# A two-layer trunk in split fp32: the order of parts, sums and products changed in four places

## The chip, the core and the metric

The kernel runs on one core of one Trainium2 chip. The metric is the device time of one execution in microseconds (us). The kernel before takes 1653.25 us, the median of three runs (1652.49 to 1653.59). The profiler records one execution by engine: PE (matrix products), ACT (activations and copies), DVE (elementwise work), POOL (here it only issues DMAs that add into memory) and SP (which issues plain loads and stores).

## The reference

The input x has 512 tokens of 1024 numbers, in fp32. Two layers follow one another:

```python
# layer i, mixer i mod 2
x += 1/2 * ffn_a(rms_norm(x)); x += mixer(rms_norm(x)); x += 1/2 * ffn_b(rms_norm(x))
# ffn: (silu(x @ Wg) * (x @ Wu)) @ W_out, inner width 2816
# mixer 0: recurrent: (gelu(y) * rg_lru(conv4(r))) @ w_out, with y, r = split(x @ w_in)
# mixer 1: spatial gating: (u * (w_s @ rms_norm(v) + b_s)) @ w_out, with u, v = split(gelu(x @ w_in))
# at the end: rms_norm(x)
```

Four feed-forward blocks and two mixers make up nearly all of the work. All of their weight products are 512 tokens by 1024 or by 2816.

## The kernel before

**Split numbers.** A product in fp32 is made of three products in fp32r, a format of fewer bits. Each operand is cut into a high part (`hi` for activations, `whi` for weights) and a low part (`lo`, `wlo`): ACT writes the high part as a copy, and DVE subtracts it from the original to get the low part. Lines 362, 363 and 364 issue the three matmuls of one 128x128 block of activations and 512 columns of weights.

**Seven products for eight.** `seven` (L334) multiplies blocks of 2 by 2 by the method of seven products, P1, P2, P5, P6, P3, P7 and Q4. Each needs one left operand out of A11, A12, S1, S2, S4, S3 and A22 (the S are sums of blocks) and one right operand, a weight block or a sum of blocks. Products add up in PSUM banks named A, B, C and Q: P1, then P6 and P7, use A; P2 uses B; P5 and P3 use C; Q4 uses Q in the output products. Each bank pair is emptied by ACT or DVE before the next product that starts in it anew. Every product is done in cuts, two or so halves of the inner dimension; product and cut together are a "sub", written P6_0 and P6_1 below.

**Weights.** A weight block is loaded by SP into a `raw` tile (`Raw.fetch`, one of 8 buffers). Sums of blocks are made in two ways. POOL can issue an accumulating DMA that adds a second block from memory onto the raw tile (`Raw.add`, L136). This is done either as `plus`, two subs after the load, from the list `pending`, or as `then`, right behind the tile's split, when the tile is used again for the next sum. Or DVE adds another raw tile onto it (`Sub.add`, `tile`), one instruction of 128x1024. A POOL DMA waits in POOL's queue until the tile is there and its last reader is done, and POOL issues strictly in order.

**Order.** The loop at the end of the kernel goes through the subs. For each it runs pending accumulations, hooks set for that sub ("pre", "mid", "rest"), the splits of weights up to three subs ahead, new loads, the matmuls, and the "end" and "late" hooks. Engine queues follow this program order; an instruction that waits holds up all behind it on its engine.

**Left operands.** `left_blocks` (L627) sets the steps of a group: the transposes `e` of a quarter (PE, L264) a number of subs later (`lag`), the evacuation of PSUM into an SBUF tile `a` and its split; then the sums S2, S4, S3 on DVE. `Group.direct` (L285) makes high and low parts straight from PSUM, half by half: hi, lo, hi, lo.

**Opening.** The kernel begins with a pair of 128-wide column blocks done plainly (`pair_plain`), while x is squared and summed for the first norm; `rt`, the norm's scale, is made by ACT and DVE. Then follows the first chunk (`chunk`, sub 8 on), whose B banks come from the two auxiliary banks, which the transposes share. Its c1 (P1 + P2) is added by DVE from bank B, which frees the auxiliary banks.

**Output products.** `out_blocks` (L559) does an output product with the residual addition. Its `parts` hooks make hi and lo of S4 and the like a number of subs ahead of their product (`lead`, 2 as a rule). In the recurrent mixer the order is P1, P5, P2 for either cut, P6, P3 for either cut, then P7 and Q4 for both. `FinalNorm` (L792) gives the order of the very last output product and joins the final norm to it; P3's two cuts are joined there.

Of the kernel before, what the change touches and what calls it, by code (L numbers as in the profile page):

```python
# [13 lines left out]
P = 128  # L14
# [38 lines left out]
def trunk(ctx: ExitStack, tc: tile.TileContext, a: dict, out: bass.AP):  # L53
# [57 lines left out]
    class Raw:  # L111
# [1 line left out]

        halves = False

        def __init__(self, src, shape, plus=None):
            self.src, self.shape, self.plus, self.uses, self.done = src, shape, plus, 0, 0

        def turn(self):
            self.uses += 1  # L120
# [2 lines left out]
        def load(self):  # L123
            _, k, c = self.shape
            t = rawp.tile([P, 1024], F32, tag="raw", name=nm("raw"))
            self.v = t[:, : k * c].rearrange("p (k c) -> p k c", k=k)
            live.add(self)
            self.fetch()
            if self.plus is not None:
                pending.append((now[0] + 2, self))  # L130

        def fetch(self):
            nc.sync.dma_start(out=self.v, in_=self.src)
# [68 lines left out]

    raws = []

    def raw_of(src, shape, plus=None):
        raws.append(Raw(src, shape, plus))
        return raws[-1]

    subs = []
# [35 lines left out]
    class Group:  # L245
# [39 lines left out]
        def direct(self, name, ps, gains):  # L285

            hi, lo = self.hl[name] = slot(F32R, "hi")[:, : self.n * H], slot(F32R, "lo")[:, : self.n * H]
            for q, g in enumerate(gains):
                c = slice(q * H, (q + 1) * H)
                act(hi[:, c], ps[:, c], AF.Copy, scale=g)  # L290
                stt(lo[:, c], ps[:, c], g, f32(hi[:, c]), ALU.mult, ALU.subtract)

        def stage(self, n, name, src, gains=None, parts=True, where=None, direct=0):
# [40 lines left out]
    def seven(block, cuts, left, w, posts, order=None, own=False, apart=False, joined=None, spare=bank):  # L334

        bk, raw, held = {}, {}, []
        banks = dict(BANK, Q4=("Q", True)) if apart else BANK

        def mm_of(prod, ci):
            name, fresh = banks[prod]
            pairs = cuts[ci]

            def mm(sub):
                if fresh and ci == 0:
                    for s in range(2):  # L350
                        bk[name, s] = (spare if name == "B" else bank)(name)[:, :w]
                if prod == joined and ci == 0:
                    held.extend((sub, q, i) for q, i in enumerate(pairs))
                    return
                for s in range(2):
                    ps = bk[name, s]
                    k = {} if fresh else dict(skip_group_check=True)
                    for sb, q, i in (held if prod == joined else []) + [(sub, q, i) for q, i in enumerate(pairs)]:
                        zh, zl = left(prod, i, s)
                        wh, wl = sb.hi[:, q, :], sb.lo[:, q, :]  # L360
                        end = i == cuts[-1][-1]
                        nc.tensor.matmul(ps, zh, wh, start=fresh and i == 0, stop=False, **k)  # L362
                        nc.tensor.matmul(ps, zl, wh, start=False, stop=False, **k)  # L363
                        nc.tensor.matmul(ps, zh, wl, start=False, stop=end, **k)  # L364
                    if ci == len(cuts) - 1 and prod in posts:
                        posts[prod](s, ps)
            return mm

        order = order or [(p, ci) for p in ORDER for ci in range(len(cuts))]

        def far(ci):
            return own and order.index(("P6", ci)) - order.index(("P5", ci)) >= 4

        for prod, ci in order:
            def new(k, n, plus=None):
                b = lambda k, n: block(k, n, cuts[ci])
                return raw_of(b(k, n), [P, len(cuts[ci]), w], plus and b(*plus))

            tile = then = tile_then = None
            if prod == "P1":  # L380
                r = raw[11, ci] = new(0, 0)
            elif prod == "P2":
                r = new(1, 0)
            elif prod == "P5":
                if own:
                    raw[11, ci] = new(0, 0, (0, 1))
                    if far(ci):
                        then = block(1, 1, cuts[ci])
                else:
                    tile = raw[12, ci] = new(0, 1)  # L390
                    tile_then = block(1, 1, cuts[ci])
                r = raw[11, ci]
            elif prod == "P6" and far(ci):
                r, then = raw[11, ci], block(1, 0, cuts[ci])
            elif prod == "P6":
                r, tile, then = raw[11, ci], new(1, 1), block(1, 0, cuts[ci])
                raw[22, ci] = tile
            elif prod == "P3":
                r = new(1, 1) if far(ci) else raw[22, ci]
            elif prod == "P7":  # L400
                r = new(0, 1, (1, 1)) if own else raw[12, ci]
            else:
                r = raw[11, ci]
            subs.append(Sub(r, mm_of(prod, ci), None, tile, then, tile_then))
        return order

# [149 lines left out]
                hook(n + 4, "pre", lambda: self.take(1))  # L556


    def out_blocks(w, k0, groups, scale, norm=None, order=None, own=False):  # L559

        n = [g for g in groups]
        cuts, bases, i, r = [], {}, 0, k0
# [57 lines left out]
        for i, (prod, ci) in enumerate(order):  # L620
            if prod in ("P3", "P6", "P7", "Q4"):
                lead = 6 if ends and prod == "P3" else 4 if isinstance(norm, TileNorm) and prod in ("P7", "Q4") else 3 if 1 in n else 2
                hook(at0 + i - lead, "mid", lambda ci=ci, name=LEFT[prod]: gs[ci].parts(name))
        return gs

# [27 lines left out]
        return left_of(lambda: S.z)  # L653


    def chunk(w_in, f0, nt, group, spare=bank):

        w = nt * P
        c1, c2, c3, c5, ht = {}, {}, {}, {}, {}

        def rt(t):
            return S.rt[:, t : t + 1]

        def new(d, s, name):
            d[s] = slot(name=name)[:, :w]
            return d[s]

        def p1(s, ps):
            act(new(c1, s, "c1"), ps, AF.Copy)

        def p2(s, ps):
            tt(c1[s], c1[s], ps, ALU.add)
            hook(now[0] + 1, "mid", lambda: act(c1[s], c1[s], AF.Silu, scale=rt(s)))

        def p5(s, ps):
            act(new(c5, s, "c5"), ps, AF.Copy)

        def p6(s, ps):
            act(new(c2, s, "c2"), ps, AF.Copy)

        def p3(s, ps):
            tt(c2[s], ps, c2[s], ALU.subtract)
            stt(c2[s], c2[s], rt(s), c1[s], ALU.mult, ALU.mult)
            ht[s] = c2[s]
            if s == 1:
                left_blocks(group, ht, 0)

        def p7(s, ps):
            act(new(c3, s, "c3"), ps, AF.Copy)
            hook(now[0] + 1, "mid", lambda: tt(c5[s], c5[s], c3[s], ALU.subtract))  # L690

        def q4(s, ps):
            s4 = slot(name="s4")[:, :w]
            act(s4, ps, AF.Silu, scale=rt(2 + s))
            stt(c5[s], c5[s], rt(2 + s), s4, ALU.mult, ALU.mult)
            ht[2 + s] = c5[s]
            if s == 1:
                left_blocks(group, ht, 1)

        seven(in_block(w_in, lambda n: n * DFF + f0 * P, w), [[0, 1], [2, 3]], x_left(), w,  # L700
              dict(P1=p1, P2=p2, P5=p5, P6=p6, P3=p3, P7=p7, Q4=q4), spare=spare)

    def pair_plain(w_in, f0, group, first=False):

# [31 lines left out]
        def post(half):  # L736
            for s in range(2):
                ps, t = st[half, s], 2 * half + s
                if t not in ht:
                    silu(half, s)  # L740
                o = slot(name="h")[:, :w]
                stt(o, ps[:, w:], S.rt[:, t : t + 1], ht[t], ALU.mult, ALU.mult)
                ht[t] = o
            left_blocks(group, ht, half, 4 if first else 2)

        at0 = len(subs)
        for i, (half, left) in enumerate(((0, "A12"), (0, "A11"), (1, "A22"), (1, "A21"))):
# [27 lines left out]
    def ffn(w_in, w_out, norm):  # L775
        f0 = 0
        for i, sizes in enumerate(FF_PARTS):
            groups, p0 = [], f0
            for n in sizes:
# [3 lines left out]
                    f0 += 2  # L783
                else:
                    groups.append(Group(n // 2))
                    chunk(w_in, f0, n, groups[-1], aux if len(subs) == 8 else bank)
                    f0 += n
            gs = out_blocks(w_out, p0, [g.n for g in groups], 0.5, norm if i == len(FF_PARTS) - 1 else None, own=True)
            gs.update(enumerate(groups))
# [2 lines left out]
    class FinalNorm:  # L792

        ORDER = [(p, ci) for p in ("P1", "P2", "P5", "P6", "P7", "Q4", "P3") for ci in range(2)]

        def __init__(self):
            self.gain, self.q, self.m, self.s = {}, {}, {}, {}
# [95 lines left out]
    def recurrent(w_in, w_out, norm):  # L895
# [132 lines left out]
        for i, at in enumerate(((11, 12, 15), (13, 14, 16))):  # L1028
            for fn, n in zip((groups[i].s2, groups[i].s4, groups[i].s3), at):
                hook(y0 + n, "pre", fn)  # L1030

        def y_post(c, ps):
            ym[c] = ps
# [31 lines left out]
        order = [(p, ci) for ci in range(2) for p in ("P1", "P5", "P2")]  # L1065
        order += [(p, ci) for ci in range(2) for p in ("P6", "P3")]
        order += [(p, ci) for p in ("P7", "Q4") for ci in range(2)]
        gs = out_blocks(w_out, 0, [2, 2], 1.0, norm, order, own=True)
        gs.update(enumerate(groups))


# [358 lines left out]
                         (4, "rest", lambda: (value(0, "A21"), value(1, "A21")))):  # L1430
        hook(n, phase, fn)
    squares(4, "rest", "A11")
    squares(4, "rest", "A12")
    squares(5, "rest", "A22")
    squares(5, "rest", "A21")
    rstd(6, (0, "rest"), (0, "rest"), (1, "pre"))
    first.rest(1, None)
    hook(20, "end", vec_rest_t)
# [50 lines left out]
```

## Time and profile before

| | us |
|---|---|
| median of three runs | 1653.25 |
| profiled execution | 1653.5 |
| its span | 1651.7 |
| PE busy | 1621.3 (98%) |
| DVE busy | 1361.2 (82%) |
| ACT busy | 1033.6 (63%) |
| POOL busy | 214.1 (13%) |

The span runs from the first to the last instruction that the profiler records; the rest of the execution's time lies around it. Busy shares are means over the whole span. A wait's row gives an engine's total idle time ahead of a kind of instruction, how many times, and the longest. A row of the timeline gives start, duration, engine, source line, operation, and what it writes and reads; in square brackets stand the idle time just before it and what ended it. Matmul durations overlap: the step from start to start is the time that one takes.

HBM moves 165 GB/s on average, and the clock of PE was 0.995 of its full rate.

### The profile page before, as it was taken

What the parts mean: (1) busy time and instruction counts of PE and PEld (TensorE: products, weight loads), DVE (VectorE), ACT (ScalarE), POOL (GpSimd) and SP (SyncE); (2) the same over time, 40 slices, a digit from 0 to 9 for tenths busy, and PEclk for the clock granted to TensorE, in tenths of its full rate; (3) what the DMA queues carried; (4) which work ended last, traced back from release to release, by engine and by line L of the source; (5) the groups of instructions that cost most, each with busy time, mean ns of one, the idle gap of its engine ahead of it and who ended that gap; (6) DMA issues with size and microseconds to landing.
All of it is one profiled execution on the core that took longest, in us unless ns stands there. A gap on an engine that the chain in (4) does not pass through costs nothing.

```text
span 1651.7 us, 20816 instructions
## 1 busy us (share of the span) xinstructions
PE 1621.3 (98%) x7475; PEld 1334.7 (81%) x7475; DVE 1361.2 (82%) x1821; ACT 1033.6 (63%) x1501; POOL 214.1 (13%) x194
## 2 busy tenths in 40 slices
PE   9899999999999999999999999999999999999997
PEld 7688888888878888888888888888788888888885
DVE  6898897887798797877987978778866888879777
ACT  6656556667867556556775565566774865665655
POOL 1111111200010111111101111112101011121110
PEclk9999999999999999999999999999999999999999
DMA  5667966853373876876838768769864557686683
GB/s 211 148 167 177 217 156 165 210 146 102 90 179 92 183 184 174 207 169 161 203 86 191 170 171 208 175 163 217 193 165 104 152 119 187 166 207 168 157 205 79
DMA packets 161560, 273.54 MB, mean 166 GB/s; under 512 B 11328, under 2 KB 37552, under 8 KB 161456
## 3 DMA queue, kind: packets, MB, share of 16 engines
q1 hardware_dynamic: 113856, 182.74, 35.8%
q0 software_dynamic: 45808, 87.63, 31.7%
q10 hardware_dynamic: 1792, 1.84, 0.4%
q8 instruction: 59, 0.97, 0.2%
q14 instruction: 45, 0.37, 0.1%
HBM read 270.07 MB, written 2.10 MB: 165 GB/s over the span
## 4 chain that ended last, share of the span: by engine, by line
PE 87%; DVE 6%; ACT 4%; issue 1%; DMA 1%; SPq 0%; ACTq 0%; DVEq 0%
PE A L362 13%; PE A L363 13%; PE A L364 13%; PE C L363 7%; PE C L364 7%; PE C L362 7%; PE p L727 4%; PE e L264 3%; PE B L362 3%; PE B L364 3%; PE B L363 3%; DVE wlo L87 2%; PE Q L364 1%; PE Q L362 1%; PE Q L363 1%
## 5 line engine op out<-in xcount | busy, mean ns | idle before, releaser
L96 ACT ACTIVATE whi<-raw 128x1024 fp32r<-128x1024 f32 (+1 forms) x530 | 547.0, 1033 | 416.4 <-PE A L363 114.5
L87 DVE TENSOR_TENSOR wlo<-raw,whi 128x1024 fp32r<-128x1024 f32 (+1 forms) x531 | 631.1, 1191 | 207.1 <-ACT whi L96 205.7
L362 PE MATMUL A<-whi,hi 128*128 128x512 f32 x984 | 392.1, 398 | 4.4 <-DVE x L93 4.4
L364 PE MATMUL A<-wlo,hi 128*128 128x512 f32 x984 | 384.9, 391 | 0.0
L363 PE MATMUL A<-whi,lo 128*128 128x512 f32 x984 | 384.5, 391 | 0.2 <-DVE lo L87 0.2
L362 PEld LDWEIGHTS A<-whi,hi 128*128 128x128 f32 x984 | 185.2, 188 | 41.3 <-issue 4.8
L362 PE MATMUL C<-whi,hi 128*128 128x512 f32 x544 | 213.8, 393 | 4.4 <-ACT hi L96 4.4
L364 PEld LDWEIGHTS A<-wlo,hi 128*128 128x128 f32 x984 | 185.1, 188 | 40.3
L363 PEld LDWEIGHTS A<-whi,lo 128*128 128x128 f32 x984 | 185.5, 189 | 37.8 <-DVE lo L87 1.2
L363 PE MATMUL C<-whi,lo 128*128 128x512 f32 x544 | 214.0, 393 | 1.8 <-DVE lo L87 1.5
L364 PE MATMUL C<-wlo,hi 128*128 128x512 f32 x544 | 213.2, 392 | 1.2 <-DVE wlo L87 1.2
L136 POOL DMA_DIRECT2D raw<-in_ffn_w_in_dram x80 | 96.4, 1205 | 750.4 <-DVE raw L87 558.6
L136 POOL DMA_DIRECT2D raw<-in_ffn_w_out_dram x72 | 83.0, 1156 | 390.3 <-DVE wlo L87 155.0
L87 DVE TENSOR_TENSOR raw<-raw,raw 128x1024 f32<-128x1024 f32 (+1 forms) x107 | 128.2, 1199 | 0.5
L87 DVE TENSOR_TENSOR lo<-a,hi 128x512 fp32r<-128x512 f32 (+1 forms) x188 | 122.6, 659 | 3.7 <-ACT hi L96 3.1
L362 PEld LDWEIGHTS C<-whi,hi 128*128 128x128 f32 x544 | 103.0, 189 | 26.9 <-ACT hi L96 5.5
L363 PEld LDWEIGHTS C<-whi,lo 128*128 128x128 f32 x544 | 102.9, 189 | 26.3 <-DVE lo L87 5.1
L364 PEld LDWEIGHTS C<-wlo,hi 128*128 128x128 f32 x544 | 102.9, 189 | 23.0 <-DVE wlo L87 1.7
L96 ACT ACTIVATE hi<-a 128x512 fp32r<-128x512 f32 (+1 forms) x188 | 112.5, 600 | 13.0 <-DVE a L87 10.8
L96 ACT ACTIVATE c<-A 128x512 f32<-128x512 f32 x126 | 74.1, 594 | 57.0 <-PE A L364 56.4
L362 PE MATMUL B<-whi,hi 128*128 128x512 f32 x272 | 109.0, 401 | 0.0
L364 PE MATMUL B<-wlo,hi 128*128 128x512 f32 x272 | 106.5, 391 | 0.6 <-DVE wlo L87 0.6
(170 smaller groups left out, 2202.9 us busy)
## 6 DMA issues: line engine op xcount, KB each, us to landing
raw<-in_ffn_w_in_dram SPq DMA_DIRECT2D x160, 512.0 KB, 4.5
raw<-in_ffn_w_out_dram SPq DMA_DIRECT2D x100, 512.0 KB, 5.4
raw<-in_ffn_w_in_dram POOLq DMA_DIRECT2D x80, 512.0 KB, 7.5
raw<-in_ffn_w_out_dram POOLq DMA_DIRECT2D x60, 512.0 KB, 7.7
raw<-in_sg_w_in_dram SPq DMA_DIRECT2D x18, 512.0 KB, 5.1
raw<-in_rec_w_in_dram SPq DMA_DIRECT2D x16, 512.0 KB, 3.9
raw<-in_ffn_w_in_dram SPq DMA_DIRECT2D x30, 256.0 KB, 4.0
raw<-in_ffn_w_out_dram SPq DMA_DIRECT2D x20, 256.0 KB, 4.8
```

Of the source, the lines that this page charges most:

```text
L87: nc.vector.tensor_tensor(out=o, in0=x, in1=y, op=op)
L96: nc.scalar.activation(out=o, in_=x, func=f, **k)
L136: nc.gpsimd.dma_start(out=self.v, in_=src, accum_op=ALU.add)
L264: nc.tensor.transpose(ps[:, o : o + P], src(q, s), ident)
L362: nc.tensor.matmul(ps, zh, wh, start=fresh and i == 0, stop=False, **k)
L363: nc.tensor.matmul(ps, zl, wh, start=False, stop=False, **k)
L364: nc.tensor.matmul(ps, zh, wl, start=False, stop=end, **k)
L727: nc.tensor.matmul(bank_of(half, s), z, (sub.lo if m == 2 else sub.hi)[:, q, :], start=left[2] == "2" and (h, q, m) == (0, 0, 0), stop=lef ...
```

## The change

The program does the same arithmetic, apart from the order of some sums of weight blocks. Six edits:

1. `Group.direct` writes both high halves first, then both low halves.
2. The last output product of the kernel goes P1, P2, P6, P5, P7, Q4, P3 in place of P1, P2, P5, P6, P7, Q4, P3. Its sums of weights are built to suit: P6 takes a fresh block (0,0) and adds a tile that holds (0,1) + (1,1); P5 goes on with P1's tile plus (0,1); Q4 goes on with P6's; P7 is the tile; P3 loads (1,1) anew. The number of loads and of DVE additions there is the same.
3. In the first chunk, P5 and P7 get tiles of their own: (0,0) and (0,1) are loaded again, and POOL accumulates (0,1) and (1,1) onto them. Two loads and two accumulating DMAs are added, two DVE additions of 128x1024 go.
4. The squares of x in the opening move: A12 from step 4 to 5, A22 and A21 from step 5 to 6.
5. The transposes of the first pair's group come one sub later (`lag` 5 for 4).
6. In the recurrent and part of the spatial output product, P7's accumulation is queued six (or five) subs after its load rather than two, the pending list is kept sorted, and in the recurrent one hi and lo for P3_0 are made a sub earlier (`soon`).

```diff
@@ class Raw
-        def __init__(self, src, shape, plus=None):
+        def __init__(self, src, shape, plus=None, wait=2):
...
             if self.plus is not None:
-                pending.append((now[0] + 2, self))
+                pending.append((now[0] + self.wait, self))
+                pending.sort(key=lambda p: p[0])
@@ Group.direct
-            for q, g in enumerate(gains):
-                c = slice(q * H, (q + 1) * H)
+            cs = [(slice(q * H, (q + 1) * H), g) for q, g in enumerate(gains)]
+            for c, g in cs:
                 act(hi[:, c], ps[:, c], AF.Copy, scale=g)
+            for c, g in cs:
                 stt(lo[:, c], ps[:, c], g, f32(hi[:, c]), ALU.mult, ALU.subtract)
@@ seven
+        def again(ci):
+            return own and order.index(("P5", ci)) - order.index(("P1", ci)) >= 6
...
             if prod == "P1":
                 r = raw[11, ci] = new(0, 0)
+                if again(ci):
+                    then = block(0, 1, cuts[ci])
...
             elif prod == "P5":
-                if own:
+                if again(ci):
+                    pass
+                elif own:
                     raw[11, ci] = new(0, 0, (0, 1))
...
+            elif prod == "P6" and joined:
+                r, tile, then = new(0, 0), new(0, 1, (1, 1)), block(1, 0, cuts[ci])
+                raw[6, ci], raw[12, ci] = r, tile
...
             elif prod == "P3":
-                r = new(1, 1) if far(ci) else raw[22, ci]
+                r = new(1, 1) if far(ci) or joined else raw[22, ci]
             elif prod == "P7":
-                r = new(0, 1, (1, 1)) if own else raw[12, ci]
+                r = raw[12, ci] if joined or not own else new(0, 1, (1, 1), 6 - ci if far(ci) else 2)
             else:
-                r = raw[11, ci]
+                r = raw[6 if joined else 11, ci]
@@ out_blocks
+                lead = soon.get((prod, ci), lead)
@@ chunk
-              dict(P1=p1, P2=p2, P5=p5, P6=p6, P3=p3, P7=p7, Q4=q4), spare=spare)
+              dict(P1=p1, P2=p2, P5=p5, P6=p6, P3=p3, P7=p7, Q4=q4), own=first, spare=aux if first else bank)
@@ pair_plain
-            left_blocks(group, ht, half, 4 if first else 2)
+            left_blocks(group, ht, half, 5 if first else 2)
@@ FinalNorm
-        ORDER = [(p, ci) for p in ("P1", "P2", "P5", "P6", "P7", "Q4", "P3") for ci in range(2)]
+        ORDER = [(p, ci) for p in ("P1", "P2", "P6", "P5", "P7", "Q4", "P3") for ci in range(2)]
@@ recurrent
+        soon = {("P3", 0): 3}
...
-        gs = out_blocks(w_out, 0, [2, 2], 1.0, norm, order, own=True)
+        gs = out_blocks(w_out, 0, [2, 2], 1.0, norm, order, own=True, soon=soon)
@@ opening
     squares(4, "rest", "A11")
-    squares(4, "rest", "A12")
-    squares(5, "rest", "A22")
-    squares(5, "rest", "A21")
+    squares(5, "rest", "A12")
+    squares(6, "rest", "A22")
+    squares(6, "rest", "A21")
```

More of the change, by code (lines that the diff above doesn't have):

```diff
@@ L114, in trunk @@
         halves = False
-        def __init__(self, src, shape, plus=None):
-            self.src, self.shape, self.plus, self.uses, self.done = src, shape, plus, 0, 0
+        def __init__(self, src, shape, plus=None, wait=2):
+            self.src, self.shape, self.plus, self.wait, self.uses, self.done = src, shape, plus, wait, 0, 0
         def turn(self):
@@ L203, in trunk, with raw_of @@
     raws = []
-    def raw_of(src, shape, plus=None):
-        raws.append(Raw(src, shape, plus))
+    def raw_of(src, shape, *plus):
+        raws.append(Raw(src, shape, *plus))
         return raws[-1]
@@ L372, in far, with new @@
             return own and order.index(("P6", ci)) - order.index(("P5", ci)) >= 4
+        def again(ci):
+            return own and order.index(("P5", ci)) - order.index(("P1", ci)) >= 6
         for prod, ci in order:
-            def new(k, n, plus=None):
+            def new(k, n, plus=None, wait=2):
                 b = lambda k, n: block(k, n, cuts[ci])
-                return raw_of(b(k, n), [P, len(cuts[ci]), w], plus and b(*plus))
+                return raw_of(b(k, n), [P, len(cuts[ci]), w], plus and b(*plus), wait)
             tile = then = tile_then = None
@@ L556, in quarter, with out_blocks @@
                 hook(n + 4, "pre", lambda: self.take(1))
-    def out_blocks(w, k0, groups, scale, norm=None, order=None, own=False):
+    def out_blocks(w, k0, groups, scale, norm=None, order=None, own=False, soon={}):
         n = [g for g in groups]
@@ L653, in x_left, with chunk @@
         return left_of(lambda: S.z)
-    def chunk(w_in, f0, nt, group, spare=bank):
+    def chunk(w_in, f0, nt, group, first=False):
         w = nt * P
@@ L785, in ffn @@
                     groups.append(Group(n // 2))
-                    chunk(w_in, f0, n, groups[-1], aux if len(subs) == 8 else bank)
+                    chunk(w_in, f0, n, groups[-1], len(subs) == 8)
                     f0 += n
```

## The prediction

> **What bounds the kernel now.** I read the page first, then the waits of TensorE, then the rows around each long wait.
>
> ```profile
> PE 1621.3 (98%) x7475; PEld 1334.7 (81%) x7475; DVE 1361.2 (82%) x1821; ACT 1033.6 (63%) x1501; POOL 214.1 (13%) x194
> PE 87%; DVE 6%; ACT 4%; issue 1%; DMA 1%; SPq 0%; ACTq 0%; DVEq 0%
> ```
>
> PE is busy 1621.3 of 1651.7 us, and the change takes no matmul away. Only the 30.4 us without PE work, and stretches in which matmuls run slowly, can be won. The waits of PE say where they lie:
>
> ```profile
> PE e L264 <- DVE c L87: 6.3, 1, 6.3
> PE C L362 <- ACT hi L96: 4.4, 3, 2.6
> PE A L362 <- DVE x L93: 4.4, 1, 4.4
> PE C L363 <- DVE lo L87: 1.5, 4, 0.8
> PE C L364 <- DVE wlo L87: 1.2, 1, 1.2
> ```
>
> Columns: total, times, longest. Four places hold nearly all of it: the opening (40 to 61 us), the recurrent mixer's output product (478), the spatial mixer's output product (1193 to 1199) and the last product (1622). Rows of PE there:
>
> ```profile
> 49.49 0.40 PE L364 MATMUL C<-wlo,hi 128*128 128x512 f32 x1
> 56.22 0.69 PE L264 MATMUL e<-ident,h 128*128 128x128 f32 x2 [6.33 <-DVE c L87]
> ...
> 478.47 0.50 PE L362 MATMUL C<-whi,hi 128*128 128x512 f32 x1 [2.59 <-ACT hi L96]
> 479.81 0.65 PE L363 MATMUL C<-whi,lo 128*128 128x512 f32 x1 [0.84 <-DVE lo L87]
> 480.26 0.63 PE L364 MATMUL C<-wlo,hi 128*128 128x512 f32 x1
> 480.69 0.63 PE L362 MATMUL C<-whi,hi 128*128 128x512 f32 x1
> ...
> 1626.31 0.47 PE L362 MATMUL A<-whi,hi 128*128 128x512 f32 x1 [4.39 <-DVE x L93]
> ```
>
> Matmuls start 0.227 us apart in ordinary stretches. After the pause at 478 they start 0.427 apart (480.26 to 480.69), and the page of windows gives a granted clock of 0.50 for 55 to 60 us. So each long wait costs the wait and about 1.8 us more: nine matmuls by 0.20.
>
> Two waits are made by a queue rather than by work:
>
> ```profile
> 466.25 2.44 POOL L136 DMA_DIRECT2D raw<-in_rec_w_out_dram  x2 [9.20 <-DMA raw<-in_ffn_w_in_dram]
> ...
> 476.84 1.06 ACT L96 ACTIVATE whi<-raw 128x1024 fp32r<-128x1024 f32 x1 [7.94 <-DMA raw<-in_rec_w_out_dram]
> 477.80 0.61 ACT L96 ACTIVATE hi<-a 128x512 fp32r<-128x512 f32 x1
> ...
> 1191.70 0.47 ACT L96 ACTIVATE hi<-e,vec 128x256 fp32r<-128x256 f32 x1 [1.32 <-DVE lo L93]
> 1192.07 0.62 ACT L96 ACTIVATE hi<-a 128x512 fp32r<-128x512 f32 x1
> ```
>
> **The change, part by part.**
>
> **Opening** (own loads in the first chunk, squares moved, transposes a step later). P1 of the chunk starts at 33.29 and P6 at 61.43: 28.1 us for 72 matmuls by 0.227 (16.3) and six transposes (0.7). So 11.1 us are lost: 8.2 in waits (0.21, 0.42, 1.24, 6.33), the rest in slow matmuls. The 6.33 is the transposes' wait for the two auxiliary banks, which P2's sums hold until DVE's c adds, and DVE is busy without a break from 37.7 to that point:
>
> ```profile
> 40.62 1.22 DVE L87 TENSOR_TENSOR raw<-raw,raw 128x1024 f32<-128x1024 f32 x1
> 44.88 1.22 DVE L87 TENSOR_TENSOR raw<-raw,raw 128x1024 f32<-128x1024 f32 x1
> 55.49 1.27 DVE L87 TENSOR_TENSOR c<-c,B 128x512 f32<-128x512 f32 x2
> ```
>
> The two block sums shown go to DMA: 2 x 1.14 = 2.3 us off the queue. The moved squares let the splits of the chunk's first two weights start ahead on ACT, so DVE's split and lo at 34.42 and 35.56 (1.7 us, and 1.5 of waiting before them) no longer stand ahead of rt, which comes at about 34.2 instead of 37.8. That would put the c adds at 55.5 - 2.3 - 3.6 = 49.6; one microsecond of waits for PE and ACT comes back in the new order, so 50.6, done at 51.8. P5's second half now stands ahead of the transposes on PE, so PE works until about 49.6 and then waits about 1.6 for the bank, and about 1.3 for ACT to empty it before the next transposes. The loss falls from 11.1 to about 3: gain 8.0. If a half-clock stretch remains, 1.8 less; if the waits fall under it, 1 more: 6 to 9. The cover of the two more loads and two more accumulating DMAs: DMA share is 0.00 to 0.27 from 30 to 45 us, and SP's queue and POOL's have nothing else there; issued at 23 to 25, they are needed at 38, and the slowest landing I found anywhere took 11.5. Their cost is nothing; without the cover, each microsecond of lateness is one on ACT's queue.
>
> The Trainium skill ("TensorE: Matmul & The Clock Gate", HAM oscillation) says that the clock halves only after an idle gap of some 3.4 us. By that the two gaps left here would cost no slow stretch. The trace is stricter: 2.59 and 0.84 us of gap, with a matmul between, did it at 479.81. By the page the sum is as above, by the row 1.8 less.
>
> **Recurrent output.** Twelve C matmuls should have ended at 475.72 + 12 x 0.227 = 478.44; they ended at 484.02, so 5.6 are lost. Cause: the POOL queue. P6_1's accumulating DMA could go at 464.6, when DVE had ended the split of P5_1, but stands behind P7_1's, which waits for its own load (landed 465.7). It goes at 466.98 and lands at 476.74, 9.75 later. ACT's whi waits 7.94 for it, and the hi that PE needs stands behind whi. Now P7's sums are issued two to four steps later, so P6_1's leaves near 464.6 and lands at 472 to 474 (7.25 to 9.75), and the hi and lo come ahead of that split in both queues. Either alone frees most of it. But P7_0, P7_1 and Q4's sums go later: P7_1's behind Q4_0's wait for DVE (469.6), landing near 480, with PE at P7_1 near 486 less the gain, its split wanted two to three steps (5 to 8 us) before. That margin is about nothing. I take 5.0; ends 5.6 (all of it) and 0 (a new wait as long, at P7 or Q4).
>
> **Hi ahead of lo in parts from PSUM.** Queue order is unchanged on each engine. In the spatial output ACT waits 1.32 and 1.33 for DVE's lo between the halves, with PE's hi behind it; PE loses 0.81 + 0.22 and 1.03 + 0.23 there. The new wait is lo 0 for hi 1, at most 0.37 us (a 128x256 hi), with DVE's lo for PE behind it. So not all of 2.3 is won: 1.8, ends 0.8 and 2.7. In the opening the same edit frees ACT between halves, inside the estimate above.
>
> **The last product.** 24 C matmuls (5.4 us) now lie between P6 and P7, which share the A banks. The 4.39 goes, and the slow clock behind it (12 matmuls took 4.42 for 2.72), 6.2 with the hand-over. What is late next is DVE. From 1605.76 to P7_0's lo the new order has six splits of 1.14, sixteen of 0.60 and one of 0.1: 16.5 us, so 1622.3; the two block sums, now earlier, fill 1.4 of idle time and push 0.9: 1623.2, against PE ready at 1621.8. Gain 6.2 - 1.6 = 4.6, if no DMA is late. One probably is. P6's second sum tile is loaded and then accumulated upon; the load in that place was issued at 1590.65 and landed at 1599.70, and accumulating DMAs around it take 5.7 to 11.5. So it is whole at 1605.5 to 1608, some at 1611, while DVE comes to its add at 1603.0, and everything of DVE stands behind. I take 2.6 of stall, as DMA is idle of other loads then: gain 2.0; ends 4.6 (no stall) and -3.6 (landed at 1611.2, 8.2 of stall).
>
> Sum: 8.0 + 5.0 + 1.8 + 2.0 = 16.8. The profiled execution took 1653.5 (span 1651.7), 0.25 over the median of 1653.25, so the kernel comes to 1636.5.
>
> **Rivals.**
> - The end and the recurrent output go without any wait: 8.0 + 5.6 + 1.8 + 4.6 = 20: 1633. For: the DMA queues are nearly empty at the end (0.00 share from 1621). Against: the 9.05 us load and 11.49 us accumulation in just that place.
> - The recurrent stall returns as a wait for P7_1's or Q4's sum: 16.8 - 5.0: 1641.5. For: the margin of about nothing; against: SP issues only two loads (472.25, 472.67) between 470 and 482.
> - The opening's transposes keep waiting, because the c adds depend on something that I placed too early: gain 3 instead of 8, 1641.5. With the one above: 1646.5.
> - Slower: the chain load, accumulation, add in the last product. The queue decides: DVE stands at the second add, ACT's split behind it, and PE runs dry. To undo 14.8 + 4.6 = 19.4 us the tile has to come 19.4 us after 1603, at 1622.4. The longest rows (10.21 and 11.49) in series put it at 1612. For: nothing in the trace; against: just that. Slower by over 0.2%: from 1625.8 on.
>
> A rule of the Trainium skill bears on this one ("SBUF — State Buffer", Who interferes with whom): POOL's descriptor generation can be starved by DVE instructions in two-port modes. No run here shows it; POOL's issues took 1.20 us with DVE full.
>
> - The change does nothing: only if all four waits return elsewhere.
>
> **How the numbers follow.** Forecast 0.45; no wait at all 0.14; recurrent wait back 0.16; opening little 0.12; both 0.04; nothing 0.03; slower 0.06. The bounds of the terms put the likeliest case at 1633 to 1640. The range leaves out the 1646.5, the nothing and the slower case (0.13) and reaches one microsecond below 1633 for the opening's better end and to 1644 for the rival cases with a worse end: 1631.5 to 1644. 0.2% (3.3 us) is what a measurement here can tell; all but the last two cases are beyond it: faster 0.91, same 0.03, slower 0.06.
>
> **What would show it.** Opening: P6 of the chunk starts near 53.4, no wait over 2 us at the transposes, c adds near 50.6. Recurrent: no PE wait over 1 us between 475 and 500, and POOL issuing P6_1's sum near 464. Spatial: ACT's two waits of 1.3 gone. End: no wait at P7; instead DVE waiting 2 to 3 us for a DMA near the first block sums. The prediction fails if a PE wait of over 3 us stands at P6 or P7 of the last product, or at P7 or Q4 of the recurrent one.

## The result, and the profile after

The changed kernel takes 1636.15 us (median of four, 1635.55 to 1636.91) against 1653.42 for the kernel before in the same session: a ratio of 0.9897, 95% interval 0.9880 to 0.9914. The forecast was 1636.5. The profiled execution has a span of 1634.8 us, 16.9 less than before.

The page of the changed kernel gives PE as the bound still, with nearly the same work:

```profile
PE 1615.5 (99%) x7475; PEld 1331.8 (81%) x7475; DVE 1357.6 (83%) x1819; ACT 1032.4 (63%) x1501; POOL 216.6 (13%) x196
```

Where the time went can be read off PE almost exactly, since long stretches of the two kernels are the same. I matched the starts of the same PE block in the two traces; the difference is constant to 0.15 us over hundreds of microseconds and moves in four places only. The shift is the start after less the start before:

| stretch (time before) | PE block | before | after | shift | gained here | forecast |
|---|---|---|---|---|---|---|
| opening | second A block after the chunk | 72.70 | 64.44 | -8.26 | 8.3 | 8.0 |
| recurrent output | A (P6_1), 484.4 | 484.38 | 470.50 | -13.88 | 5.6 | |
| the same, at its end | A (P7_1), 493.7 | 493.66 | 483.71 | -9.95 | 1.7 in all | 5.0 |
| spatial output and gate | u, 1213 | 1212.95 | 1200.26 | -12.69 | 2.7 | 1.8 |
| last product | C (P3) | 1638.89 | 1620.81 | -18.08 | 5.4 | |
| end of span | | 1651.7 | 1634.8 | -16.9 | 4.2 in all | 2.0 |

So the total came out as forecast, but not every term did: the recurrent output won 3.3 us less, the end 2.2 more, the spatial output 0.9 more. The waits of PE in the changed kernel that lie in the four places (total, times, longest):

```profile
PE A L365 <- ACT hi L96: 1.7, 1, 1.7
PE e L265 <- DVE c L87: 1.3, 1, 1.3
PE e L265 <- ACT a L96: 1.1, 1, 1.1
PE e L265 <- DVE x L93: 0.8, 2, 0.6
PE C L366 <- DVE lo L87: 0.8, 2, 0.6
PE A L366 <- DVE lo L87: 0.7, 1, 0.7
PE Q L366 <- DVE lo L87: 0.5, 1, 0.5
```

None is over 2 us, and no slow matmul follows any of them. But the first line is new: it stands at P7_0 of the recurrent output. The rows of the opening in the changed kernel, first of PE, then of DVE:

```profile
51.20 0.44 PE L265 MATMUL e<-ident,h 128*128 128x128 f32 x2 [1.34 <-DVE c L87]
51.39 0.49 PE L365 MATMUL A<-whi,hi 128*128 128x512 f32 x1
51.72 0.39 PE L366 MATMUL A<-whi,lo 128*128 128x512 f32 x1
...
55.70 0.44 PE L265 MATMUL e<-ident,h 128*128 128x128 f32 x2 [1.06 <-ACT a L96]
```

```profile
34.10 0.16 DVE L87 TENSOR_TENSOR rt<-rt,ti 128x4 f32<-128x4 f32 x1
50.46 1.27 DVE L87 TENSOR_TENSOR c<-c,B 128x512 f32<-128x512 f32 x2
```

The wait of 6.33 us is 1.34, the c additions begin at 50.46 (forecast 50.6), rt is there at 34.1 (forecast 34.2). P6 already starts at 51.39, ahead of the 53.4 that I gave, since its first half goes before the second pair of transposes. The recurrent output, rows of POOL, ACT and PE:

```profile
456.65 2.44 POOL L137 DMA_DIRECT2D raw<-in_rec_w_out_dram  x2 [9.10 <-DVE wlo L87]
461.33 2.44 POOL L137 DMA_DIRECT2D raw<-in_rec_w_out_dram  x2 [2.24 <-DVE wlo L87]
```

```profile
474.93 1.06 ACT L96 ACTIVATE whi<-raw 128x1024 fp32r<-128x1024 f32 x1 [3.38 <-PE e L265]
```

```profile
479.37 0.47 PE L365 MATMUL A<-whi,hi 128*128 128x512 f32 x1 [1.69 <-ACT hi L96]
```

In program order the POOL pairs are P6_1's and P7_0's sums at 456.65, Q4_0's and P7_1's at 461.33. P6_1's landed at 462.5, long before it was needed. P7_1's was issued at 462.06 and landed at 474.82, and ACT's split of P7_1 begins at 474.93. The row blames the transposes, and by this trace alone either could be meant: they were issued at 474.31 and took 0.60 us. An experiment below decides for the sum: with the sum at 471.14 the same split begins at 471.25, before the transposes, 0.11 us behind the landing as here. From that split on ACT has next to no idle time (gaps of 0.03), and the last thing that PE waits for, P7_0's high part, comes at the end of that row of work, at 479.36. DVE's split and, behind it, DVE's first addition that empties the A banks end only a little earlier, at 479.23:

```profile
478.54 1.28 DVE L93 SCALAR_TENSOR_TENSOR x<-A,x 128x512 f32<-128x512 f32 x2
478.75 0.61 ACT L96 ACTIVATE hi<-a 128x512 fp32r<-128x512 f32 x1
```

The end, DVE and PE:

```profile
1587.94 1.22 DVE L87 TENSOR_TENSOR raw<-raw,raw 128x1024 f32<-128x1024 f32 x1
1590.87 1.23 DVE L87 TENSOR_TENSOR raw<-raw,raw 128x1024 f32<-128x1024 f32 x1 [0.58 <-DMA raw<-in_ffn_w_out_dram]
```

```profile
1615.47 0.50 PE L366 MATMUL Q<-whi,lo 128*128 128x512 f32 x1 [0.53 <-DVE lo L87]
```

The second sum tile is late as forecast, but by 0.58 us, not 2.6.

### The profile page after: what moved, and what is told of

Same layout as the page of the kernel before. It is cut to its first block, busy times and chain, and to the rows that moved or that the text cites. A ratio compares the mean times of both kernels' runs of the same rounds, so it can differ in the third digit from the quotient of the medians.

```text
span 1634.8 us, 20824 instructions
## 1 busy us (share of the span) xinstructions
PE 1615.5 (99%) x7475; PEld 1331.8 (81%) x7475; DVE 1357.6 (83%) x1819; ACT 1032.4 (63%) x1501; POOL 216.6 (13%) x196
## 4 chain that ended last, share of the span: by engine, by line
PE 88%; DVE 6%; ACT 3%; issue 1%; DMA 0%; SPq 0%; DVEq 0%; ACTq 0%
PE A L365 13%; PE A L366 13%; PE A L367 13%; PE C L366 7%; PE C L367 7%; PE C L365 7%; PE p L742 5%; PE e L265 4%; PE B L365 3%; PE B L367 3%; PE B L366 3%; DVE wlo L87 2%; PE Q L367 1%; PE Q L365 1%; PE Q L366 1%
```

## The experiments

All are the changed kernel with one part taken back or altered, timed against the kernel before, which took 1653.65, 1654.21 and 1653.40 us (medians) in the three sessions. Since the same kernel differs by 0.8 us from session to session, differences under about 1 us say nothing by themselves; the shifts of PE blocks against the changed kernel are given beside the times, since they show where a difference arises.

### The three edits of the opening taken back

```diff
-              dict(P1=p1, P2=p2, P5=p5, P6=p6, P3=p3, P7=p7, Q4=q4), own=first, spare=aux if first else bank)
+              dict(P1=p1, P2=p2, P5=p5, P6=p6, P3=p3, P7=p7, Q4=q4), spare=aux if first else bank)
...
-            left_blocks(group, ht, half, 5 if first else 2)
+            left_blocks(group, ht, half, 4 if first else 2)
...
-    squares(5, "rest", "A12")
-    squares(6, "rest", "A22")
-    squares(6, "rest", "A21")
+    squares(4, "rest", "A12")
+    squares(5, "rest", "A22")
+    squares(5, "rest", "A21")
```

> The changed kernel with the opening's three edits taken back (block sums of the first chunk on DVE, squares at steps 4 and 5, transposes a step earlier); all else stays. Theory (the four places add up): the opening's 8.3 us come back, 1636.2 + 8.3 = 1644.5, with PE's wait of 6.3 us at the transposes near 56 us. Rival (the both-high-parts-first edit in the opening carries part of the gain): clearly less, 1639 to 1642, with a wait under 5 us at 56.

Measured: 1640.57 us (1639.90 to 1641.25), 4.4 slower than the changed kernel; PE behind the opening is 5.41 late, not 8.3. (Some of it is won back at P7_0 of the recurrent output, where PE waits 0.94 here and 1.69 in the changed kernel.)

```profile
52.81 0.69 PE L265 MATMUL e<-ident,h 128*128 128x128 f32 x2 [5.83 <-DVE c L87]
```

And of DVE:

```profile
34.19 0.16 DVE L87 TENSOR_TENSOR rt<-rt,ti 128x4 f32<-128x4 f32 x1
```

The total agrees with the rival: a third of the opening's gain belongs to the edit that was left in, both high parts first. With that edit alone, and the squares at their old steps, `rt` is already there at 34.19. (Its other mark, a wait under 5 us near 56, is not there: the wait is 5.83 and ends at 52.81.)

### High and low parts by halves again

```diff
-            for c, g in cs:
-                act(hi[:, c], ps[:, c], AF.Copy, scale=g)
             for c, g in cs:
+                act(hi[:, c], ps[:, c], AF.Copy, scale=g)
                 stt(lo[:, c], ps[:, c], g, f32(hi[:, c]), ALU.mult, ALU.subtract)
```

> The changed kernel with hi and lo made half by half again in parts from PSUM. Theory (the edit carries the spatial output's 2.7 us and about 2.8 of the opening's 8.3, since taking back the three other edits of the opening cost only 5.5 us on PE): 5.5 slower, 1641.7; PE's waits at the spatial C products are back (0.8 to 1.0), and P6 of the first chunk starts 2.8 later. Rival (it does nothing in the opening): 2.7 slower, 1638.9.

Measured: 1642.62 us (1641.69 to 1643.60), 6.5 slower: the largest of all the parts. (Lines of the kernel move up by one here.) PE is 4.03 late behind the opening, 3.27 behind the recurrent output (whose own wait shrinks), 5.97 behind the spatial one: 4.0 and 2.7. Rows of ACT in this kernel, and of DVE:

```profile
22.40 0.84 ACT L96 ACTIVATE hi<-e,vec 128x256 fp32r<-128x256 f32 x2 [2.55 <-DVE lo L93]
26.02 0.84 ACT L96 ACTIVATE hi<-e,vec 128x256 fp32r<-128x256 f32 x2 [0.63 <-DVE lo L93]
27.82 0.62 ACT L96 ACTIVATE junk<-x 128x512 f32<-128x512 f32 x1
```

```profile
38.12 0.16 DVE L87 TENSOR_TENSOR rt<-rt,ti 128x4 f32<-128x4 f32 x1
54.48 1.28 DVE L87 TENSOR_TENSOR c<-c,B 128x512 f32<-128x512 f32 x2
```

ACT waits for DVE between the halves here (2.55, 0.58, 0.63 and 0.58 us), so its squares start at 27.82; in the changed kernel at 23.69. The kernel before has the same waits:

```profile
21.54 0.84 ACT L96 ACTIVATE hi<-e,vec 128x256 fp32r<-128x256 f32 x2 [2.54 <-DVE lo L93]
25.17 0.84 ACT L96 ACTIVATE hi<-e,vec 128x256 fp32r<-128x256 f32 x2 [0.64 <-DVE lo L93]
37.60 0.16 DVE L87 TENSOR_TENSOR rt<-rt,ti 128x4 f32<-128x4 f32 x1
```

The changed kernel (ACT):

```profile
22.24 1.57 ACT L96 ACTIVATE hi<-e,vec 128x256 fp32r<-128x256 f32 x4 [1.00 <-PE e L265]
23.69 0.65 ACT L96 ACTIVATE junk<-x 128x512 f32<-128x512 f32 x1
```

About 4 us pass to rt (38.12 for 34.10) and to the c additions (54.48 for 50.46). And rt is no earlier here, with the squares moved, than in the kernel before, with the squares at their old steps (37.60).

### Block sums of the first chunk on DVE

The first of the three edits above alone.

> The changed kernel with the first chunk's P5 and P7 from block sums on DVE again, everything else changed. Theory (DVE's queue sets the opening): two sums of 1.14 us stand again ahead of the c additions, so these come 2.3 later, PE's wait at the transposes is 3.6 instead of 1.3, and the total is 2.3 slower, 1638.5, and up to 1640.5 if the longer wait brings slow matmuls. Rival (the accumulating loads are not faster than DVE's queue, the squares do it all): within 0.5 of 1636.2.

Measured: 1637.55 us (1636.95 to 1637.98), 1.4 slower. The c additions begin at 51.41, 0.95 later, and PE behind the opening is 0.98 late. At P7_0 of the recurrent output most of it is won back, since the wait there is 0.92, so that the span is only 0.4 longer in the profile. Between theory and rival: 0.95 of the 2.3 of work counts. DVE's queue had some waiting in the changed kernel's order (0.66 for ACT's split at 37.86), which the sums fill.

### Squares a step earlier

> The changed kernel with the squares at steps 4 and 5 again. Theory (splits stand ahead of the norm's scale in DVE's queue, then the scale comes 3.6 us later and so do the c additions): 2 to 3.6 slower, 1638 to 1640. Rival (DVE has slack there now that the two sums are gone): within 0.7 of 1636.2.

Measured: 1636.28 us (1635.91 to 1636.45). The rival holds.

```profile
34.34 0.16 DVE L87 TENSOR_TENSOR rt<-rt,ti 128x4 f32<-128x4 f32 x1
50.70 1.28 DVE L87 TENSOR_TENSOR c<-c,B 128x512 f32<-128x512 f32 x2
```

rt moves by 0.24. With the other edits in place, the moved squares are worth next to nothing.

### Transposes of the first pair a sub earlier

> The changed kernel with the first pair's transposes a sub earlier, ahead of P5's second half. Theory (2.7 us of P5's matmuls no longer cover the wait for the auxiliary banks): PE waits 4.1 instead of 1.3 at the transposes, and the next wait of 1.1 goes since ACT has more time: 1.6 slower, or 3.4 with slow matmuls after the longer wait: 1637.8 to 1639.6. Rival (the transposes are not on the path): within 0.5 of 1636.2.

Measured: 1639.50 us (1638.17 to 1639.89), 3.4 slower, 3.55 on PE behind the opening.

```profile
51.08 0.69 PE L265 MATMUL e<-ident,h 128*128 128x128 f32 x2 [4.06 <-DVE c L87]
51.42 0.78 PE L365 MATMUL C<-whi,hi 128*128 128x512 f32 x1
52.00 0.63 PE L366 MATMUL C<-whi,lo 128*128 128x512 f32 x1
52.42 0.63 PE L367 MATMUL C<-wlo,hi 128*128 128x512 f32 x1
```

The theory, with the slow matmuls: 4.06 of wait for 4.1, and then 0.43 us from start to start. This edit is worth its 2.7 us of cover and the slow stretch that the longer wait sets off.

### The old last product

```diff
-            elif prod == "P6" and joined:
+            elif prod == "P6" and joined and again(ci):
...
-                r = new(1, 1) if far(ci) or joined else raw[22, ci]
+                r = new(1, 1) if far(ci) else raw[22, ci]
...
-                r = raw[12, ci] if joined or not own else new(0, 1, (1, 1), 6 - ci if far(ci) else 2)
+                r = raw[12, ci] if not own else new(0, 1, (1, 1), 6 - ci if far(ci) else 2)
...
-                r = raw[6 if joined else 11, ci]
+                r = raw[11, ci]
...
-        ORDER = [(p, ci) for p in ("P1", "P2", "P6", "P5", "P7", "Q4", "P3") for ci in range(2)]
+        ORDER = [(p, ci) for p in ("P1", "P2", "P5", "P6", "P7", "Q4", "P3") for ci in range(2)]
```

> The changed kernel with the old order and the old sums of the last product. Theory: the end's share comes back, 4.2 us (span) of the 16.9: 1640.4, and the wait of 4.4 us at P7 with about nine slow matmuls returns. Rival (the last product gains what its PE rows gained, 5.4, and the tail's 1.2 belongs to something else): 1641.6.

Measured: 1641.05 us (1640.06 to 1641.67), 4.9 slower; the wait is back at its old length.

```profile
1613.37 0.77 PE L365 MATMUL A<-whi,hi 128*128 128x512 f32 x1 [4.39 <-DVE x L93]
```

The span is 1639.8, 5.0 longer, and PE entered the last product 0.27 earlier than in the changed kernel: the product costs 5.3 more. That is nearer the rival's 5.4 than the theory's 4.2, but not clean evidence for either, since the slow stretch starts with the second matmul here (0.42 from 1613.94 to 1614.36) and started with the third in the kernel before, and lasts longer (12 such steps for 8).

### The recurrent edits taken back, together and one by one

```diff
-                r = raw[12, ci] if joined or not own else new(0, 1, (1, 1), 6 - ci if far(ci) else 2)
+                r = raw[12, ci] if joined or not own else new(0, 1, (1, 1), 2)
...
-        soon = {("P3", 0): 3}
+        soon = {}
```

> The changed kernel with P7's sums queued two subs after their loads again and hi and lo of P3_0 as before. Theory (in the changed kernel 3.9 of the 5.6 us won at P3_0 are given back at P6_1, P3_1 and P7 for P7_1's late sum): only 1.7 us slower, 1637.9, with the 2.6 and 0.8 us waits at P3_0 back and none at P7. Rival (what is given back at P7 has nothing to do with the moved sums and stays): 5.6 slower, 1641.8.

> The changed kernel with P7's sums queued two subs after their loads again, hi and lo of P3_0 still a sub earlier. Theory (either half of the edit frees P3_0 alone; the delay of P7's sums is what makes the later wait): P6_1's sum lands near 468, its split comes just in time behind P3_0's 2.7 us of matmuls, P7_1's sum is early, and the wait of 1.7 at P7 is gone: 1634.0 to 1636.2. Rival (the POOL order is what frees the stall): at P6_1 a wait of 2 to 3 us and slow matmuls, 1638 to 1640.

> The changed kernel with hi and lo of P3_0 two subs ahead as before, P7's sums late as in the changed kernel. Theory (P6_1's sum lands near 462.5, well ahead of its split, so that what stands behind that split does not matter): 1636.2 within 0.7, no wait over 1 us at P3_0. Rival: the wait at P3_0 is back in part, 1637.5 to 1639.

Measured: both taken back 1639.16 (1638.78 to 1639.50), on PE 6.54 late at P6_1 but only 2.43 at the end of the product; the POOL order alone taken back 1637.62 (1637.21 to 1638.80), 0.95 late on PE; hi and lo's lead alone taken back 1636.76 (1635.93 to 1637.50), not late on PE (0.64 early, with a wait of 0.36 at P3_0).

Both back (PE):

```profile
470.14 0.50 PE L365 MATMUL C<-whi,hi 128*128 128x512 f32 x1 [2.69 <-ACT hi L96]
471.48 0.79 PE L366 MATMUL C<-whi,lo 128*128 128x512 f32 x1 [0.84 <-DVE lo L87]
```

Old POOL order, hi and lo early (PE):

```profile
471.71 0.33 PE L265 MATMUL e<-ident,x 128*128 128x128 f32 x1 [1.22 <-DVE x L93]
474.64 0.79 PE L366 MATMUL A<-whi,lo 128*128 128x512 f32 x1 [1.55 <-DVE lo L87]
475.23 0.63 PE L367 MATMUL A<-wlo,hi 128*128 128x512 f32 x1
475.66 0.63 PE L365 MATMUL A<-whi,hi 128*128 128x512 f32 x1
```

The first theory holds in the main: PE loses 2.43 us where 1.7 were expected, far from the rival's 5.6. Most of what P3_0 won was given back by the end of the product, and with the old order there is no wait at P7. The second falls: hi and lo ahead of the split do free P3_0, but P6_1's sum, landed at 468.6 in that kernel, then holds P6_1 itself, and DVE's additions behind its split, for which the transposes wait; its rival's slow matmuls come as well (0.43 from start to start). The third holds. So POOL's order alone does all of the work, and the earlier hi and lo add nothing to it. With POOL's old order they are worth something: 1639.16 without them, 1637.62 with them, 1.48 us on PE.

### P7_1's sum ahead of Q4_0's

```diff
-                r = raw[12, ci] if joined or not own else new(0, 1, (1, 1), 6 - ci if far(ci) else 2)
+                r = raw[12, ci] if joined or not own else new(0, 1, (1, 1), 6 - 2 * ci if far(ci) else 2)
```

> The changed kernel with one number changed: P7_1's sum is due four subs after its load instead of five, so that in POOL's queue it stands ahead of Q4_0's sum instead of behind it. Theory: it is issued near 458 instead of 462 and lands near 469 instead of 474.8; ACT's split of P7_1 no longer waits 3.4 us, DVE frees the A banks sooner, and 2 to 3.9 us come back: 1632.3 to 1634.2. Rival (P7 waits for DVE's own backlog, not for the sum): 1636, with PE's 1.7 us wait still there.

Measured: 1636.20 us (1635.22 to 1637.47). In the profiled execution the sum is issued at 457.75 and lands at 471.14, 3.7 earlier; ACT splits P7_1 at once, PE's wait at P7 is gone, and PE is 2.06 early there, at the lower end of the theory (rows of POOL and ACT):

```profile
456.30 3.68 POOL L137 DMA_DIRECT2D raw<-in_rec_w_out_dram  x3 [9.10 <-DVE wlo L87]
```

```profile
471.25 1.06 ACT L96 ACTIVATE whi<-raw 128x1024 fp32r<-128x1024 f32 x1
```

So P7_1's late sum is 2.06 of the 3.93 us that the changed kernel gives back between P6_1 and P7_1. The rest stays, as waits for DVE: 0.68 in P6_1 and 0.53 and 0.21 at the transposes behind P7_0. DVE has no idle time left there, from 457.7 to 480.8.

But the total hardly moves. PE is 2.04 early at the last product, then only 0.79. DVE's row there:

```profile
1590.07 1.23 DVE L87 TENSOR_TENSOR raw<-raw,raw 128x1024 f32<-128x1024 f32 x1 [2.17 <-DMA raw<-in_ffn_w_out_dram]
```

The second sum tile landed at 1590.05, at nearly the same time as in the changed kernel (1590.85), though everything else was 2 us earlier. Its load did start 2.38 earlier (1575.60 for 1577.98), but took 6.22 us for 5.20, and the sum 7.67 for 7.10. Most of the gain at P7 went into the stall at the end.

### P6's sum tile loaded first in the last product

```diff
-                r, tile, then = new(0, 0), new(0, 1, (1, 1)), block(1, 0, cuts[ci])
+                tile, r, then = new(0, 1, (1, 1)), new(0, 0), block(1, 0, cuts[ci])
```

> The changed kernel with P6's sum tile loaded ahead of P6's own block in the last product (two loads change places, for both cuts). Theory (the second tile's sum lands at the moment when DVE comes to it, 0.6 us late here and 2.2 where the kernel ran 2 us ahead of its loads): no DVE wait at the block sums, 0 to 0.6 faster: 1635.5 to 1636.2. Rival (P6's own block or P5's sum is late instead): up to 2 slower.

> The changed kernel with P7_1's sum ahead of Q4_0's, and P6's sum tile loaded first. Theory: the 1.7 to 2.0 us that the first won on PE at P7 are no longer lost to DVE's wait of 2.2 at the second block sum: 1634.2 to 1635.0. Rival (DVE's backlog at the end takes it whatever the DMAs do): 1636.2.

Measured: alone 1634.98 us (1634.20 to 1635.24); with P7_1's sum first 1633.95 (1633.71 to 1634.58), ratio to the kernel before 0.9880 (0.9865 to 0.9895). With both, DVE's block sums follow without a wait:

```profile
1585.83 1.22 DVE L87 TENSOR_TENSOR raw<-raw,raw 128x1024 f32<-128x1024 f32 x1
1586.97 1.22 DVE L87 TENSOR_TENSOR wlo<-raw,whi 128x1024 fp32r<-128x1024 f32 x1
1588.10 1.22 DVE L87 TENSOR_TENSOR raw<-raw,raw 128x1024 f32<-128x1024 f32 x1
```

PE is 2.1 earlier than in the changed kernel when the last product begins, 2.78 at its P3, and the span is 2.8 shorter (1632.0). The tile's order alone gives the same 0.67 in the last product; that kernel's other 0.83 arose at the recurrent output, where its wait at P7 was shorter (0.85) although nothing there was altered, as in five of the other kernels with this POOL order. This is the fastest version found; all of its runs lie below all of the changed kernel's (1635.55 and up). It bears out that the two waits belong together: removing the one at P7 pays in full only once the tile at the end comes in time.

## Why the prediction was right, point by point

**Opening: right in size, wrong in one cause.** Forecast 8.0, measured 8.3. The c additions did start 5.0 earlier, as the sum has it. But of the single edits, the squares moved them by 0.24, the sums by 0.95, and the hi-before-lo edit by 4.02, which I had called "inside the estimate above". The step that failed is that the moved squares bring rt from 37.8 to 34.2: rt came early because ACT no longer waited for DVE between halves (2.54, 0.58, 0.64 and 0.58 us in the kernel before), ahead of the squares. Five kernels separate the two edits: with the old hi and lo order rt comes at 37.60 (old squares) and 38.12 (moved), with the new one at 34.19 and 34.34 (old squares) and 34.10 (moved). With the squares moved, DVE's split no longer stands in front of rt, but ACT's squares do. I had read the rows right in front of rt and not the waits on ACT ten microseconds earlier. That 34.2 came out is luck: another edit paid a term of the same size. The later transposes were worth 3.55, their cover and the slow stretch. The four single losses (4.03, 3.55, 0.98, 0.24) sum to 8.8 for 8.3, but they are not independent: the last three taken back together cost 5.41, so that the first is worth 2.85 without them and 4.03 with them.

**The slow matmuls.** I left 1.8 us open on whether the remaining gaps of 1.6 and 1.3 would bring a slow stretch. They measured 1.34 and 1.06 and brought none. Single gaps of up to 2.1 us (2.09 and 2.12, in the opening of two of the kernels above) gave no slow stretch, and 4.06, 4.39 and 5.83 did. The Trainium skill's rule ("TensorE: Matmul & The Clock Gate", HAM oscillation), a halved clock after an idle gap of some 3.4 us, fits these single gaps. Shorter gaps close together halved the clock as well: 2.69 and 0.84 with one matmul between, in the kernel with the recurrent edits taken back, and 1.22, 0.27 and 1.55 within 4.2 us, in the one with POOL's order alone taken back (a granted clock of 0.50 from 475 to 477.5). They bear out the stricter reading of the row at 479.81.

**Recurrent output: wrong.** Forecast 5.0, measured 1.7. "That margin is about nothing" was the sentence to believe: the second rival, a wait for P7_1's sum, came true on this term. The mis-sized thing is the landing: I had it near 480, in the time of the kernel before, that is 471.7 after the opening's gain; it landed at 474.82, 12.8 us after its issue, longer than any row that I had looked at (11.5) and than any in the kernel before (11.9). That the landing sets the wait at P7 is borne out by the other eight kernels with this POOL order: where the sum took 11.94 to 12.10 us, PE waited 0.85 to 1.02, and where it took 12.67 and 12.68, PE waited 1.54 and 1.61. The second term that was missing is DVE's backlog, the 0.68, 0.53 and 0.21 of wait that are left when the sum comes early; the forecast had no price for it. The reason of the landing's length can be seen in part: over its flight, from 462 to 474.8, two to four accumulating DMAs and up to four loads were under way at a time, and the DMA engines had a share of 1.08 (220 GB/s). That this is the cause was argued, not shown: issued 4.3 us earlier, the same sum took 13.4. That either half of the edit alone would free most of it was half right: POOL's order alone does all of it, the earlier hi and lo alone 1.48 of the 2.43 us.

**Spatial output: right, undersized.** Forecast 1.8, measured 2.7. By the A block behind the two C products 2.2 are won, with one wait of 0.55 for DVE's lo left: the price that I charged for the new wait of lo behind the second hi was right in size, but with each wait removed went more than its idle time (the step behind the first, at 1192.74, was 1.19 us, 0.97 more than usual, with 0.81 idle). Another 0.5, which I had not counted, came in the A block behind, ahead of the gate's u product. Its second matmul waited for DVE's lo in the kernel before and started 0.67 after the first; now it starts 0.31 after it, without a wait:

```profile
1202.12 0.50 PE L363 MATMUL A<-whi,lo 128*128 128x512 f32 x1 [0.19 <-DVE lo L87]
```

ACT's rows show the edit at work, the pair of high halves without a wait and PE's hi directly behind:

```profile
1179.88 0.84 ACT L96 ACTIVATE hi<-e,vec 128x256 fp32r<-128x256 f32 x2
1180.60 0.65 ACT L96 ACTIVATE hi<-a 128x512 fp32r<-128x512 f32 x1
```

**The last product: right, undersized.** Forecast 2.0, measured 4.2. The stall is the term that was off: 0.58 for 2.6, as the load ahead of the sum took 5.20 us and not the 9.05 of the row that I had taken. PE gained 5.4 up to P3, and 1.2 of that was lost again in the tail, where DVE, which has no idle time between 1604.17 and 1623, reaches the last additions later than PE allows. So DVE did become what is late next, as forecast, only after P7 instead of at it.

**The range.** 1631.5 to 1644 held the time. That the forecast was met within 0.4 us is luck, owed to errors that cancel: 0.3 + 0.9 + 2.2 against 3.3.

## What to carry to other kernels

When an engine alternates with another inside a small loop (hi, lo, hi, lo), look at what stands behind the loop in its queue: here the first engine's waits of 0.6 and 2.5 us, in a place where PE was not waiting, were worth 4 us thirty microseconds later. On a queue that issues in order, moving an item back is as much a change as moving one forward: list for each item moved past another when it will be needed. And a gain upstream lasts only if what is loaded downstream lands earlier as well: here a load that started 2.4 us earlier had its sum in place only 0.8 earlier, and the place that had been just in time took most of the gain.

## What the runs showed of the hardware

An accumulating DMA of 512 KB took 5.6 to 13.5 us from issue to landing in these traces; the longest, 13.4 and 13.5, were two of four issued within 5 us. Gaps of PE that are each too short can halve its clock together: 1.22, 0.27 and 1.55 us within 4.2 us did. Where two releases lie close together, the one that a wait's row names need not be the one that counted: ACT's row at 474.93 names the transposes, while a run with the landing moved shows that it was the sum.
